# Top-2 gate dispatch on one core: the second group's first load on the scalar queue, beside the first group's last store

## The chip, the cores and the metric

The kernel runs on one core of a Trainium2 chip. The metric is the device time of one execution in microseconds; lower is better. Times before and after are medians of several runs.

## The reference

For 16 x 1024 = 16,384 tokens with 512 values each there are 8 router logits per token. The reference takes a softmax over the 8, keeps the two largest probabilities, scales them so that they sum to one, and writes the token's row twice, once times each of the two weights, the smaller first:

```python
probs = np.exp(router_logits - logits_max); probs /= probs.sum(-1, keepdims=True)
topk_indices = np.argsort(probs, axis=-1)[..., -k:]            # k = 2
topk_probs = np.take_along_axis(probs, topk_indices, axis=-1)
topk_probs = topk_probs / topk_probs.sum(-1, keepdims=True)
out = x[:, :, None, :].repeat(k, axis=2) * topk_probs[..., None]   # (16, 1024, 2, 512) float32
```

33.5 MB of x and 0.5 MB of logits are read, 67.1 MB of output are written.

## The kernel before

Tokens are laid on 128 partitions, 128 to a partition. They are cut into two groups (GROUPS = 65 and 63 tokens to a partition); a "row" below is one token on every partition. A row of x is 2 KB on a partition, a row of output 4 KB. In a group, each partition's rows lie together in memory, in x and in the output, so a transfer of n rows is one contiguous piece for each partition.

There are two big tiles in the on-chip memory. `xs` holds 65 rows of x. `osp` holds 18 rows of output. The output of a stretch is written either to `osp` or into `xs` itself, over rows of x that are used up, two places to an output row. That is why the loads of group 2 must wait for the stores of group 1 that read `xs`.

For each group the code issues loads, and then for each stretch a multiplication on VectorE and a store:

```python
LOADS = [[6, 12, 16, 31], [16, 16, 31]]
STORES = [
    [(0, 3, "osp", 0), (3, 15, "osp", 3), (18, 16, "xs", 0), (34, 15, "osp", 0), (49, 16, "xs", 33)],
    [(0, 16, "osp", 2), (16, 16, "xs", 0), (32, 15, "osp", 0), (47, 16, "xs", 32)],
]
```

An entry of STORES is first row, rows, tile and place in it. Group 1's x is at places 0 to 64 of `xs`, group 2's at 1 to 63. The first load of group 2 therefore fills places 1 to 16, the second 17 to 32, the third 33 to 63. The store (18, 16, "xs", 0) reads places 0 to 31, and the store (49, 16, "xs", 33), group 1's last, reads 33 to 64. So the first load doesn't overlap the last store, and the third load does.

The weights come from one small chain on VectorE and two sigmoids on ScalarE (`top2_weights`), early in the kernel. All loads and stores are issued from SyncE's queue (SP, queue q1), in program order, except the very first store of 3 rows, which goes over the scalar queue (ACT, queue q10). Within SP's queue, the three loads of group 2 stand behind all stores of group 1 and ahead of all stores of group 2. A multiplication that writes to place 0 of `osp` again is cut in two (FREE), since its first rows are free earlier.

Lines of the profile before: L120 is every load of x, L125 and L126 the loads of the logits, L133 the multiplication, L145 every store.

Of the kernel before, what the change touches and what calls it, by code (L numbers as in the profile page):

```python
# [1 line left out]

# [4 lines left out]

F32 = mybir.dt.float32
ALU = mybir.AluOpType
ACTF = mybir.ActivationFunctionType  # L10
P = 128


def top2_weights(nc, WA, dlt, room, logits, E):

    tt = nc.vector.tensor_tensor
    hi, lo, n = None, None, E  # L20
    while n > 1:
        n //= 2
        if hi is None:
            a, b = logits[:, :, 0:n], logits[:, :, n : 2 * n]
            nhi, nlo = room(n), b
            tt(nhi, a, b, op=ALU.max)  # L26
            tt(nlo, a, b, op=ALU.min)  # L27
        else:
            a, b = hi[:, :, 0:n], hi[:, :, n : 2 * n]
            nhi, nlo, tmp = room(n), room(n), room(n)  # L30
            tt(tmp, lo[:, :, 0:n], lo[:, :, n : 2 * n], op=ALU.max)  # L31
            tt(nlo, a, b, op=ALU.min)  # L32
            tt(nlo, nlo, tmp, op=ALU.max)  # L33
            tt(nhi, a, b, op=ALU.max)  # L34
        hi, lo = nhi, nlo
    tt(dlt, hi[:, :, 0], lo[:, :, 0], op=ALU.subtract)  # L36
    nc.scalar.activation(WA[:, :, 0], dlt, ACTF.Sigmoid, scale=-1.0)  # L37
    nc.scalar.activation(WA[:, :, 1], dlt, ACTF.Sigmoid, scale=1.0)  # L38

GROUPS = [65, 63]

LOADS = [[6, 12, 16, 31], [16, 16, 31]]
BASE = [0, 1]
# [6 lines that stand above are left out]
L = 18  # L52

FREE = [3, 2]


@with_exitstack
def kernel(
    ctx: ExitStack,
    tc: tile.TileContext,  # L60
    x: bass.AP,
    router_logits: bass.AP,
    k: bass.AP,
    out: bass.AP,
):
    nc = tc.nc
    B, S, D = x.shape
    E = router_logits.shape[-1]
    N = B * S
    assert int(k) == 2 and E == 8 and N == P * sum(GROUPS)  # L70
    M = N // P

    x_v, o_v, rl_v = [], [], []
    t0 = 0
    for n in GROUPS:
        t1 = t0 + P * n
        x_v.append(
            x.rearrange("b s d -> (b s) d")[t0:t1].rearrange("(p m) d -> p m d", p=P)
        )
        o_v.append(  # L80
            out.rearrange("b s k d -> (b s) k d")[t0:t1].rearrange(
                "(p m) k d -> p m k d", p=P
            )
        )
        rl_v.append(
            router_logits.rearrange("b s e -> (b s) e")[t0:t1].rearrange(
                "(p m) e -> p m e", p=P
            )
        )
        t0 = t1  # L90

    wpool = ctx.enter_context(tc.tile_pool(name="wpool", bufs=1))
    xs = wpool.tile([P, max(GROUPS), D], F32)
    osp = wpool.tile([P, L, 2, D], F32)
    WA = wpool.tile([P, M, 2], F32)
    dlt = wpool.tile([P, M], F32)


    flat = osp.rearrange("p l k d -> p (l k d)")
    taken = [0]  # L100

    def room(n):
        o = taken[0]
        taken[0] += M * n
        return flat[:, o : o + M * n].rearrange("p (m n) -> p m n", n=n)

    logits = room(E)

    def place(where, at, n):

        if where == "osp":
            return osp[:, at : at + n]
        return xs[:, at : at + 2 * n, :].rearrange("p (r k) d -> p r k d", k=2)

    m0 = 0
    for g, G in enumerate(GROUPS):
        x0, r = BASE[g], 0
        for n in LOADS[g]:
            tc.keep_in_program_order(
                nc.sync.dma_start(xs[:, x0 + r : x0 + r + n, :], x_v[g][:, r : r + n, :])  # L120
            )
            r += n
            if g == 0 and r == 6:
                n0 = GROUPS[0]
                tc.keep_in_program_order(nc.sync.dma_start(logits[:, :n0], rl_v[0]))  # L125
                tc.keep_in_program_order(nc.sync.dma_start(logits[:, n0:], rl_v[1]))  # L126
                top2_weights(nc, WA, dlt, room, logits, E)
        assert r == G
        for r, n, where, at in STORES[g]:
            og = place(where, at, n)  # L130
            again = where == "osp" and at == 0 and r > 0
            for a, b in [(0, FREE[g]), (FREE[g], n)] if again else [(0, n)]:
                nc.vector.tensor_tensor(  # L133
                    og[:, a:b],
                    xs[:, x0 + r + a : x0 + r + b, :]
                    .unsqueeze(2)
                    .to_broadcast([P, b - a, 2, D]),
                    WA[:, m0 + r + a : m0 + r + b, :]
                    .unsqueeze(3)
                    .to_broadcast([P, b - a, 2, D]),  # L140
                    op=ALU.mult,
                )

            queue = nc.scalar if g == r == 0 else nc.sync
            tc.keep_in_program_order(queue.dma_start(o_v[g][:, r : r + n], og))  # L145
        m0 += G


# [1 line left out]
_INS = ['x', 'router_logits', 'k']  # L150
_OUTS = [((16, 1024, 2, 512), 'float32')]

_NUMBERS = {'k': 2}


# [26 lines left out]
```

## Time and profile before

| what | value |
|---|---|
| median of 3 runs | 240.02 us (239.98 to 240.04) |
| profiled execution, its time | 240.69 us |
| its span | 238.9 us |
| VectorE busy | 141.8 us (59%) |
| ScalarE busy | 1.8 us (1%) |
| bytes moved by DMA | 101.19 MB, mean 424 GB/s over the span |
| share of sixteen DMA engines, SP's queue / ACT's queue | 97.0% / 1.5% |

The span runs from the first instruction to the last; the profiled execution's own time is 1.8 us longer. "SPq" and "ACTq" are the instruction queues of SyncE and ScalarE, and the time given for a DMA there is only its issue. The data moves later, on sixteen DMA engines that both queues share; the time "to landing" is from issue until all of the data has arrived.

### The profile page before, as it was taken

The page shows a single profiled execution, that of the slowest core. Times are in us where ns is not written, and L with a number is a line of the kernel's source. Part 1 is how long each engine was busy: PE and PEld are TensorE (multiplying, and loading weights), DVE is VectorE, ACT ScalarE, POOL GpSimd, SP SyncE. Part 2 cuts the span into 40 slices and gives each one's busy share as a digit, 9 for nine tenths or more (in the row PEclk, how much of TensorE's full clock was granted, in tenths as well). Part 3 has the DMA queues.
Part 4 walks back from the last instruction along what each step waited for, and adds up shares of the span by engine and source line. Part 5 has one row for each costly group of instructions (what it writes and reads, how often), then busy time and mean ns, then how long its engine had stood idle before and what let it go on. Part 6 is the DMA issues. An engine that isn't in the chain of part 4 may idle for free.

```text
span 238.9 us, 105 instructions
## 1 busy us (share of the span) xinstructions
DVE 141.8 (59%) x22; ACT 1.8 (1%) x3; POOL 0.2 (0%) x4
## 2 busy tenths in 40 slices
DVE  0699999980089999100000799999306999950000
ACT  2000000000000000000000000000000000000000
POOL 0000000000000000000000000000000000000000
DMA  7999998979989997989899999798989899989894
GB/s 262 439 440 430 377 544 372 494 339 494 494 362 472 406 484 339 494 351 527 351 439 439 439 433 510 340 505 362 505 373 494 384 461 395 484 350 505 362 516 176
DMA packets 2592, 101.19 MB, mean 424 GB/s; under 512 B 288, under 2 KB 416, under 8 KB 544
## 3 DMA queue, kind: packets, MB, share of 16 engines
q1 hardware_dynamic: 2448, 99.62, 97.0%
q10 hardware_dynamic: 144, 1.57, 1.5%
HBM read 34.08 MB, written 67.11 MB: 424 GB/s over the span
## 4 chain that ended last, share of the span: by engine, by line
DMA 45%; DVE 43%; SPq 0%; issue 0%; ACT 0%; DVEq 0%
DMA out_dram<-osp 27%; DVE osp L133 27%; DMA xs<-in_x_dram 15%; DVE xs L133 14%; DMA osp<-in_router_logits_dram 3%; DVE osp L26 0%; DVE osp L27 0%; DVE osp L33 0%; DVE osp L32 0%; DVE osp L34 0%; DVE osp L31 0%; SPq L125 0%; SPq L120 0%; SPq L145 0%; ACT WA L38 0%
## 5 line engine op out<-in xcount | busy, mean ns | idle before, releaser
L133 DVE TENSOR_TENSOR osp<-xs,WA 128x3072 f32<-128x3072 f32 (+5 forms) x7 | 69.3, 9907 | 62.2 <-DMA xs<-in_x_dram 36.4
L133 DVE TENSOR_TENSOR xs<-xs,WA 128x16384 f32<-128x16384 f32 x4 | 68.9, 17224 | 0.1
L26 DVE TENSOR_TENSOR osp<-osp 128x512 f32<-128x512 f32 x1 | 0.7, 693 | 8.3 <-DMA osp<-in_router_logits_dram 8.3
L37 ACT ACT_TABLE_LOAD x1 | 1.3, 1283 | 0.7 <-PEq L163 0.7
L27 DVE TENSOR_TENSOR osp<-osp 128x512 f32<-128x512 f32 x1 | 0.7, 691 | 0.0
L32 DVE TENSOR_TENSOR osp<-osp 128x256 f32<-128x256 f32 (+1 forms) x2 | 0.7, 350 | 0.0
L31 DVE TENSOR_TENSOR osp<-osp 128x256 f32<-128x256 f32 (+1 forms) x2 | 0.7, 349 | 0.0
L33 DVE TENSOR_TENSOR osp<-osp 128x256 f32<-128x256 f32 (+1 forms) x2 | 0.7, 349 | 0.0
L34 DVE TENSOR_TENSOR osp<-osp 128x256 f32<-128x256 f32 (+1 forms) x2 | 0.7, 348 | 0.0
L37 ACT ACTIVATE WA<-dlt 128x128 f32<-128x128 f32 x1 | 0.3, 315 | 10.2 <-DVE dlt L36 10.2
L36 DVE TENSOR_TENSOR dlt<-osp 128x128 f32<-128x128 f32 x1 | 0.3, 293 | 0.0
L38 ACT ACTIVATE WA<-dlt 128x128 f32<-128x128 f32 x1 | 0.3, 298 | 0.0
L163 POOL MEMSET const-bfloat16-1.0<- 128x1 bf16 x1 | 0.1, 101 | 0.0
L163 POOL MEMSET const-uint8-127<- 128x1 uint8 x1 | 0.1, 101 | 0.0
L163 POOL MEMSET const-float32-0.0<- 128x1 f32 x1 | 0.1, 98 | 0.2 <-issue 0.2
L163 POOL MEMSET const-float32-1.0<- 128x1 f32 x1 | 0.1, 98 | 0.0
## 6 DMA issues: line engine op xcount, KB each, us to landing
out_dram<-osp SPq DMA_DIRECT2D x3, 7680.0 KB, 24.4
xs<-in_x_dram SPq DMA_DIRECT2D x2, 7936.0 KB, 41.8
xs<-in_x_dram SPq DMA_DIRECT2D x3, 4096.0 KB, 35.9
xs<-in_x_dram SPq DMA_DIRECT2D x1, 3072.0 KB, 13.4
xs<-in_x_dram SPq DMA_DIRECT2D x1, 1536.0 KB, 6.1
out_dram<-osp ACTq DMA_DIRECT2D x1, 1536.0 KB, 22.2
osp<-in_router_logits_dram SPq DMA_DIRECT2D x1, 260.0 KB, 6.4
osp<-in_router_logits_dram SPq DMA_DIRECT2D x1, 252.0 KB, 6.5
```

Of the source, the lines that this page charges most:

```text
L26: tt(nhi, a, b, op=ALU.max)
L27: tt(nlo, a, b, op=ALU.min)
L31: tt(tmp, lo[:, :, 0:n], lo[:, :, n : 2 * n], op=ALU.max)
L32: tt(nlo, a, b, op=ALU.min)
L33: tt(nlo, nlo, tmp, op=ALU.max)
L34: tt(nhi, a, b, op=ALU.max)
L36: tt(dlt, hi[:, :, 0], lo[:, :, 0], op=ALU.subtract)
L37: nc.scalar.activation(WA[:, :, 0], dlt, ACTF.Sigmoid, scale=-1.0)
L38: nc.scalar.activation(WA[:, :, 1], dlt, ACTF.Sigmoid, scale=1.0)
L133: nc.vector.tensor_tensor(og[:, a:b], xs[:, x0 + r + a : x0 + r + b, :] .unsqueeze(2) .to_broadcast([P, b - a, 2, D]), WA[:, m0 + r + a : ...
L163: nc = _bacc.Bacc("TRN2", target_bir_lowering=False, num_devices=1)
```

## The change

The first load of group 2 (16 rows, places 1 to 16 of `xs`) is issued from the scalar queue instead of SP's. A dependence is added by hand: it begins when the store ahead of the last one of group 1, (34, 15, "osp", 0), has landed. All other instructions keep their queues and their order.

```diff
     m0 = 0
+    stores = []
     for g, G in enumerate(GROUPS):
         x0, r = BASE[g], 0
         for n in LOADS[g]:
-            tc.keep_in_program_order(
-                nc.sync.dma_start(xs[:, x0 + r : x0 + r + n, :], x_v[g][:, r : r + n, :])
-            )
+
+            queue = nc.scalar if g == 1 and r == 0 else nc.sync
+            load = queue.dma_start(xs[:, x0 + r : x0 + r + n, :], x_v[g][:, r : r + n, :])
+            if queue is nc.scalar:
+                tc.add_manual_dep(
+                    load.ins,
+                    stores[-2].ins.name,
+                    mybir.DependencyInfo(
+                        mybir.DependencyClass.Sync, mybir.DependencyReason.DATA
+                    ),
+                    reason="begin when the store ahead of the last has landed",
+                )
+            tc.keep_in_program_order(load)
             r += n
...
             queue = nc.scalar if g == r == 0 else nc.sync
-            tc.keep_in_program_order(queue.dma_start(o_v[g][:, r : r + n], og))
+            stores.append(queue.dma_start(o_v[g][:, r : r + n], og))
+            tc.keep_in_program_order(stores[-1])
         m0 += G
```

## The prediction

> **What bounds the kernel now.** I read the page first for which resource is full, then the waits of the engines, then the waits of SP's own queue, then the DMA issues one by one, and last the trace's single DMA packets. The page:
>
> ```profile
> span 238.9 us, 105 instructions
> DVE 141.8 (59%) x22; ACT 1.8 (1%) x3; POOL 0.2 (0%) x4
> DMA  7999998979989997989899999798989899989894
> DMA packets 2592, 101.19 MB, mean 424 GB/s; under 512 B 288, under 2 KB 416, under 8 KB 544
> q1 hardware_dynamic: 2448, 99.62, 97.0%
> q10 hardware_dynamic: 144, 1.57, 1.5%
> ```
>
> The row to look at is the DMA row: nearly full in every slice. q1 is SP's queue and q10 ACT's; together their packets took 98.5% of sixteen engines' time. VectorE is busy for 59% only. There are 18 transfers of 128 partitions, and 2592 / 18 = 144 packets each: 128 data packets, one for each partition (I call them lines), and 16 end marks of 4 bytes. So each of the 16 DMA engines has 8 lines and a mark of every transfer.
>
> I put the packets, in order of start, onto sixteen engines. They then lie back to back on every engine from 1.81 us to 237.71 us, without a gap: 235.9 us from first to last, of which the mean engine is busy for 235.5. The same line always takes the same time: 65,536 bytes (a 16-row store) 2.418 us, 61,440 bytes (15 rows) 2.267, 63,488 bytes (a 31-row load) 2.342, 32,768 bytes (a 16-row load) 1.213. The end is therefore the sum of the lines' durations, and a wait of VectorE shortens nothing unless a DMA engine runs dry because of it. The biggest wait of VectorE is the one that the change is aimed at:
>
> ```profile
> DVE osp L133 <- DMA xs<-in_x_dram: 36.4, 1, 36.4
> DVE osp L133 <- DMA out_dram<-osp: 25.3, 2, 13.6
> ```
>
> The first row is VectorE waiting for the second group's first load. The timeline of that stretch shows why it is long:
>
> ```profile
> 79.31 0.33 SPq L145 DMA_DIRECT2D out_dram<-osp  x1
> 96.57 0.33 SPq L145 DMA_DIRECT2D out_dram<-xs  x1
> 96.95 26.58 SPq L120 DMA_DIRECT2D xs<-in_x_dram  x3
> 132.90 17.23 DVE L133 TENSOR_TENSOR osp<-xs,WA 128x16384 f32<-128x16384 f32 x1 [36.36 <-DMA xs<-in_x_dram]
> 150.16 0.34 SPq L145 DMA_DIRECT2D out_dram<-osp  x1
> ```
>
> The load is issued at 96.95 and lands 35.86 us later, since two stores stand ahead of it in the same queue. The third load of that row waits on SP for the last store of group 1:
>
> ```profile
> SPq L120 <- DMA out_dram<-xs: 24.2, 1, 24.2
> ```
>
> By packets, the last store's lines run from 102.86 to 122.76, the first load's to 132.5, the second's to 142.1, the third's from 141.5 to 161.6. No engine is idle in between.
>
> **The change, part by part.** *Issue.* One 16-row load leaves SP and comes to ACT, 128x8192, 4.19 MB either way; bytes, lines and marks stay. An issue costs 0.33 to 0.37 us of the issuing queue. On SP, one issue less ahead of the second load, at 97 us, with 6 us of lines queued: nothing. On ACT the load stands behind the activations and the small store of 16.12, and waits there for the store issued at 79.31. Nothing is queued behind it on ACT, so this wait holds up no one.
>
> *When it starts.* The store of 79.31 lands 24.4 us later:
>
> ```profile
> out_dram<-osp SPq DMA_DIRECT2D x1, 7680.0 KB, 24.4
> ```
>
> That is 103.7; the load is issued by 104.1. By then the last store is on the engines, 7 to 8 of its 8 lines still to go.
>
> *How the two queues share.* The trace has one such case, the small store on ACT's queue beside loads on SP's:
>
> ```profile
> 16.12 0.37 ACTq L145 DMA_DIRECT2D out_dram<-osp  x1
> out_dram<-osp ACTq DMA_DIRECT2D x1, 1536.0 KB, 22.2
> ```
>
> With equal shares of bytes 1.57 MB would pass in 2 x 1.57 / 0.424 = 7.4 us; it took 22.2. By packets, each engine first finished three lines of SP's queue (the current one and two more, first ACT line at 19.7 to 21.1), and then took one line of each queue in turn: 0.46 us of ACT's, 1.21 or 2.34 us of SP's. So shares go by line, and the longer line gets more. Here the load has the short line, 1.21 us, and the store the long one, 2.42.
>
> The Trainium skill, "DMA: Bandwidth & Descriptors", section "Queues, rings and completion order", says that an engine drains a whole packet of a ring, some 9 to 17 descriptors typically, before it switches rows. By that rule the load's 8 lines and its mark would pass in one go and land near 120; this trace's turns of one line speak against it. The same page's section "Issuing engines are not separate DMA queues" speaks against the change altogether: a second issuer saves sequencer time only. By either rule the sum below is the same, since they shift lines and remove none.
>
> *Landing of the load.* On one engine, the store's lines start at 102.9; three go first, to 110.1. Then five turns of 1.21 + 2.42 = 3.63 us, to 128.3: the store's data is out. Three load lines are left, now in turn with the second load's lines of 1.21 us: 6 lines, 4.85 us less the part after the mark, to about 134.3. The landing came 0.9 us after this engine's mark before (132.81 against 131.88), so 135.2; with two lines first instead of three, 134.0. VectorE starts at 134 to 135.3, *later* than 132.9 by 1 to 2.5 us. The load is spread out beside the store and not moved ahead of it.
>
> *What hangs on that.* The store of group 2's first part is issued at 151.3 to 152.6 instead of 150.16. The engines need it when the third load's lines end, at 160.7 on the first engine; a queue that is ready starts within 1.1 us of the issue (0.72 to 1.81 at the kernel's start). At least 7 us of cover remain. After that the order on SP's queue is as before, and VectorE's next wait, for this store's landing at 181.23, moves by nothing.
>
> *The third load.* It waits on SP for the last store of group 1, which now lands at about 130.5 instead of 123.2, being shared. Queued behind it on SP are group 2's stores, which are not ready before 151. The engines need the third load when the first two are through, at 141.5 as before, because store and loads together are the same lines. The cover shrinks from 18 us to 11; an issue and its start cost 1.4. Whatever the arbitration, the second load lies behind the store in SP's queue, so 9.7 us (8 x 1.213) of it are always left when the store is out. If this cover were gone, each microsecond of lateness would be one at the end.
>
> *The turns themselves.* What is left is whether lines get longer where reads and writes alternate. Lines longer than usual occur in four places of the trace. At the start, 0.57 us for the mean engine, unchanged. At 18 to 28 us, where the small store runs beside the 16-row load: 0.54 us for the mean engine, 0.74 for the engine that ends last. Most of it lies on the load line before the first store line (0.25) and on the load's last line (0.24). Near 158, where the third load gives way to a store: 0.48, and 0.75 on the engine that ends last. Near 45, the same switch: 0.04. In between, from 28 to 38 us, four turns of 2.34 and 0.46 us cost nothing at all, and the switch from store to load at 122 costs nothing. The new turns begin from a store (row of 122: 0), go through six to eight load lines between store lines, and end in loads. From the 16-row load's inner lines at 20 to 25 us, 0.016 us a line, eight make 0.13. The bounds are 0 and 0.54 + 0.13 = 0.67 for the mean engine, up to 0.9 for the slowest. Below zero: the 0.48 near 158 could vanish if the engines come to that switch in another order. I take 0.25: the inner lines at 0.13 and half of one 0.24 switch.
>
> *The sum.* The profiled execution took 240.69, its span is 238.9, so 1.8 lies around it. Issue 0, landing of the load 0 (covered), third load 0 (covered), turns +0.25: 240.94 for a profiled one. The median of the runs is 240.02, 0.67 below the profiled execution; so 240.3. A measurement of this kernel can tell about 0.2%, 0.48 us, from no change; the bounds of "same" are 239.54 and 240.50.
>
> **The rivals.** The forecast, a load that lands no earlier, all of it hidden, and turns at +0.25, has a chance of 0.56.
>
> *The turns cost more (slower).* Lines that alternate pay at each switch what 18 to 28 us shows at its two bad places, about 0.24. With five or six turns that is 1.2 to 1.4: 241.3. For it: the only 16-row load that was mixed with stores has its mean line at 1.280 instead of 1.213. Against it: the four free turns from 28 to 38 us. It decides from about 0.1 us a turn (five turns make 0.48). With the milder sum of 0.67 to 0.9 the time is 240.7 to 240.9. Chance 0.32.
>
> *A gain (faster).* If the engines took the load's eight lines in one go from 110.1, it would be in 9.7 us later and land near 121, and VectorE would start 12 us earlier. That alone gives 240.0, since no engine was idle. A gain beyond 0.48 needs the long lines near 158 to go as well, with nothing paid in the turns: 240.02 - 0.48 = 239.5, at best 239.3 by the slowest engine. Chance 0.12.
>
> *The load isn't beside the store.* The dependence could hold it until the store is through; then it lands no later than 142 and VectorE's store still comes at 159.5, just in time: 240.0, within "same". The order of instructions shows it on ACT behind the store of 79.31, so this is not likely.
>
> **How the numbers follow.** Same 0.56, slower 0.32, faster 0.12. The predicted time is that of the forecast, 240.3. The range goes from the gain's 239.5 up to the dearer turns' 241.3; what is left out are turns dearer still and a dry queue. The forecast's own range is 240.0 to 240.7.
>
> **What would show it.** Right: in the profile after, VectorE's wait for the load is 37 to 39 us; ACT's load is issued near 104 and lands 30 to 31 us later; the third load is issued on SP near 130.5; the DMA row stays full, and q10 carries 5.77 MB. The lines sum to 235.5 to 236.2 for the mean engine. Wrong: a landing near 121 (the engines drain a queue in one go), a gap between lines near 141 or 160 (a cover that I overrated), or lines of 1.213 us that become 1.4 and more in the stretch from 110 to 130.

## The result and the profile after

The changed kernel took 241.39 us (median of 8 runs, 240.76 to 242.64) against 239.98 us before (8 runs, 239.85 to 240.04): a ratio of 1.0059 with a 95% interval of 1.0046 to 1.0072, so 0.6% slower. Its fastest run is slower than any run of before, and its times scatter over 1.9 us where those of before stay within 0.2. The forecast was 240.3, the range ended at 241.3.

The profiled execution took 241.52 us. Its page shows the same nearly full DMA row, with the load's 4.19 MB moved from q1 to q10:

```profile
span 239.7 us, 107 instructions
DMA  7999897979989897999989999989899999898984
DMA packets 2592, 101.19 MB, mean 422 GB/s; under 512 B 288, under 2 KB 416, under 8 KB 544
q1 hardware_dynamic: 2304, 95.42, 92.6%
q10 hardware_dynamic: 288, 5.77, 5.6%
```

The two shares add to 98.2% of a span that is 0.8 us longer; before it was 98.5%. In time that is the same: the lines' durations sum to 235.48 us for the mean engine, and to 235.52 before. So the mean DMA engine was busy no longer than before, and yet the last of them ended later.

VectorE's waits, and the timeline of the stretch around the load:

```profile
DVE osp L144 <- DMA xs<-in_x_dram: 39.4, 1, 39.4
DVE osp L144 <- DMA out_dram<-osp: 23.2, 2, 13.5
```

```profile
96.39 0.33 SPq L156 DMA_DIRECT2D out_dram<-xs  x1
96.77 34.88 SPq L122 DMA_DIRECT2D xs<-in_x_dram  x2
103.70 0.35 ACTq L122 DMA_DIRECT2D xs<-in_x_dram  x1
135.72 17.23 DVE L144 TENSOR_TENSOR osp<-xs,WA 128x16384 f32<-128x16384 f32 x1 [39.36 <-DMA xs<-in_x_dram]
152.97 0.34 SPq L156 DMA_DIRECT2D out_dram<-osp  x1
```

The load is issued from ACT at 103.70, and VectorE starts the second group at 135.72, 2.8 us later than before (132.90). SP's row of two loads ends at 96.77 + 34.88 = 131.65: the third load was issued then, 10 us before the engines needed it. The store of 152.97 also came in time. None of these waits reaches the end.

What does reach the end is in the single packets (their times, here and below, are counted from a point 0.07 to 0.09 us ahead of the timeline's zero). On thirteen engines the last data packet ends between 236.4 and 236.8 us, a little sooner than before (236.6 to 237.4 for fifteen engines there, 237.7 for the last). Three engines end at 238.1, 238.3 and 238.6. Their lines, with the start of each in us (S a 16-row store line, L a 16-row load line, L31 a line of the third load):

```
one of the thirteen   S 103.0  S 105.4  L 107.8               S 109.0  L 111.4 ... L31 158.0 (2.34)  S 160.4
late engine 1         S 103.0  S 105.4  S 107.8 (3.06)  L 110.9 (1.53)  S 112.4 ... L31 159.0 (3.20)  S 162.2
late engine 2         S 102.9  S 105.3  S 107.8 (3.19)  L 110.9         S 112.2 ... L31 158.8 (3.31)  S 162.1
late engine 3         S 103.1  S 105.5  S 107.9 (3.17)  L 111.1         S 112.3 ... L31 158.9 (3.57)  S 162.5
```

In brackets are durations; the usual ones are 2.42 (S), 1.21 (L) and 2.34 (L31). Thirteen engines turned to the load after two lines of the last store. Three took a third store line first, and this line was under way when the others changed from storing to loading and back. It took 0.64 to 0.77 us too long. From then on these engines are late, so their last line of the third load is under way when the others turn to stores at 160.4, and it takes 0.86 to 1.23 too long. For late engine 3 that is 0.75 + 1.23 = 1.98 us; it ended 2.0 us after the median engine. Between the two places, nothing is longer on any engine. Of the thirteen, six have 0.04 to 0.19 extra on their last load line near 158, where in the trace of before all sixteen had 0.16 to 0.75.

The execution's time is the last engine's end plus a constant: 241.52 - 238.56 = 2.96 after, 240.69 - 237.70 = 2.99 before, 2.96 to 2.98 in ten of the eleven profiles below, and 3.10 in that of e11. So the mean engine says nothing of the time; the slowest does.

### The profile page after: what moved, and what is told of

The parts are those of the page before. It is cut to its first block, busy times and chain, and to the rows that moved or that the text cites. A ratio compares the mean times of both kernels' runs of the same rounds, so it can differ in the third digit from the quotient of the medians.

```text
span 239.7 us, 107 instructions
## 1 busy us (share of the span) xinstructions
DVE 141.8 (59%) x22; ACT 1.8 (1%) x3; POOL 0.2 (0%) x4
## 4 chain that ended last, share of the span: by engine, by line
DMA 53%; DVE 35%; issue 0%; SPq 0%; ACT 0%; ACTq 0%; DVEq 0%
DMA out_dram<-osp 36%; DVE osp L144 27%; DMA xs<-in_x_dram 13%; DVE xs L144 7%; DMA osp<-in_router_logits_dram 3%; DVE osp L26 0%; DVE osp L27 0%; DVE osp L33 0%; DVE osp L32 0%; DVE osp L31 0%; DVE osp L34 0%; SPq L136 0%; SPq L122 0%; ACT WA L38 0%; DVE dlt L36 0%
## 5 line engine op out<-in xcount | busy, mean ns | idle before, releaser
L31 DVE TENSOR_TENSOR osp<-osp 128x256 f32<-128x256 f32 (+1 forms) x2 | 0.7, 350 | 0.0
## 6 DMA issues: line engine op xcount, KB each, us to landing
xs<-in_x_dram ACTq DMA_DIRECT2D x1, 4096.0 KB, 31.9
```

## The experiments

The theory that I took from this: the load's lines reach the engines while these choose what to do next, some engines turn a line later than the rest, and whoever is out of step at a change of direction between loading and storing pays (SPLIT, later OUT OF STEP). Its rivals: every turn between a store line and a load line costs something (TURNS), or the coming of a second queue costs one long line, whatever the lines are (ARRIVAL).

| kernel | us, median (range, runs) | before beside it | ratio, 95% interval | profiled: last engine's end / median engine's |
|---|---|---|---|---|
| e1 the change again | 241.50 (240.86 to 242.85, 10) | 240.15 | 1.0062, 1.0039 to 1.0085 | 239.3 / 236.6 |
| e2 load ahead, on SP | 240.55 (240.27 to 241.42, 10) | 240.15 | 1.0016, 1.0002 to 1.0030 | 237.8 / 236.7 |
| e3 second load on ACT | 240.14 (239.86 to 241.56, 10) | 240.15 | 0.9996, 0.9976 to 1.0015 | 237.2 / 236.7 |
| e4 change, four activations | 242.37 (239.67 to 242.69, 10) | 240.15 | 1.0052, 1.0015 to 1.0088 | 239.7 / 236.6 |
| e5 before, first store on SP | 240.50 (240.39 to 240.71, 11) | 240.10 | 1.0014, 1.0005 to 1.0023 | 237.7 / 237.0 |
| e6 e4 with first store on SP | 240.27 (240.09 to 240.58, 11) | 240.10 | 1.0001, 0.9992 to 1.0011 | 237.1 / 236.9 |
| e7 change, eight activations | 242.41 (242.38 to 242.58, 4) | 240.10 | 1.0091, 1.0077 to 1.0105 | 239.5 / 236.5 |
| e8 change without dependence | 242.48 (242.18 to 243.40, 4) | 240.10 | 1.0098, 1.0077 to 1.0120 | 239.2 / 237.0 |
| e9 before again | 240.02 (239.82 to 240.28, 10) | 240.21 | 0.9988, 0.9976 to 1.0000 | 237.0 / 236.6 |
| e10 change with first store on SP | 241.19 (240.25 to 241.54, 10) | 240.21 | 1.0030, 1.0015 to 1.0045 | 238.6 / 237.1 |
| e11 store beside the store | 240.45 (240.34 to 242.23, 10) | 240.21 | 1.0022, 0.9999 to 1.0045 | 237.4 / 236.9 |

**e1, the change again.** No edit.

> The changed kernel once more, for a second profile. Three theories. SPLIT: the load's lines reach the engines while these choose their next line; some engines get them one line later than the rest, go on storing while the others already read, lose about 0.7 us there, are then late, and lose about 1 us more where the third load gives way to a store near 158. The end is set by those few engines. Expected: again a few engines (not the same number as before, perhaps) with one line longer by 0.6 to 0.8 us near 108, the same engines with a last load line longer by 0.8 to 1.3 near 158, ends of the engines spread over 1.5 us or more; time 240.7 to 242.7, scattered. TURNS: every turn between a store line and a load line costs something on every engine; expected long lines all through 108 to 130 us on all engines, and a steady time. ARRIVAL: the coming of a second queue's lines costs each engine one long line, whatever the lines are; expected long lines near 108 on most engines.

```profile
104.16 0.35 ACTq L122 DMA_DIRECT2D xs<-in_x_dram  x1
```

Again slow and scattered; the profiled execution took 242.29. Here it was a single engine. It came 0.7 us late to the last store (first line at 103.7 instead of 103.0) and turned after two store lines, the other fifteen after three. Its store line of 113.3 took 0.52 too long, two more 0.10 each, and its last load line 1.19, from 159.7, 0.6 to 1.0 us before the others turned to stores. The fifteen others had no long line after 47 us. TURNS and ARRIVAL, which want long lines on all or most engines, are against this.

**e2, the load ahead of the last store, in SP's own queue.**

```diff
+            if g == 1 and r == 0:
+                r += n
+                continue
...
+            if g == 0 and r + n == G:
+                tc.keep_in_program_order(
+                    nc.sync.dma_start(xs[:, 1 : 1 + LOADS[1][0], :], x_v[1][:, 0 : LOADS[1][0], :])
+                )
             tc.keep_in_program_order(queue.dma_start(o_v[g][:, r : r + n], og))
```

> The same load moved ahead of group 1's last store in SP's own queue, none of it on ACT. VectorE then starts group 2 near 114 instead of 132.9. SPLIT: in one queue all engines have the same order of lines, none can be a line off; 239.9 to 240.3, steady, engines' ends within 1.1 us of each other as before the change. TURNS: one more switch from loads to a store than before, 240.0 to 240.5. ARRIVAL: no second queue there, 240.0. If an idle VectorE were what bounds the kernel, this would be the fastest of all, by up to 10 us; none of the three expects that.

```profile
85.52 0.34 SPq L150 DMA_DIRECT2D xs<-in_x_dram  x1
96.44 0.33 SPq L152 DMA_DIRECT2D out_dram<-xs  x1
...
113.78 17.23 DVE L136 TENSOR_TENSOR osp<-xs,WA 128x16384 f32<-128x16384 f32 x1 [17.37 <-DMA xs<-in_x_dram]
```

In this timeline VectorE starts group 2 at 113.78, 19 us earlier than before, and the kernel gains nothing: 240.55, 0.16% slower. That settles that VectorE's long wait was covered, and that the aim of the change brings nothing here even where it is reached. But one queue for all is not without late engines: the engine that ends last, 1.1 us after the median one, lost 0.53 and 0.16 us near 105 and 112, around the added switch, 0.26 at 134 and 0.30 at 159.

**e3, the second load on ACT instead, after the last store.**

```diff
-            queue = nc.scalar if g == 1 and r == 0 else nc.sync
+            queue = nc.scalar if g == 1 and r == 16 else nc.sync
...
-                    stores[-2].ins.name,
+                    stores[-1].ins.name,
```

> The first load of group 2 is back on SP; the second one (also 16 rows) goes over ACT, when group 1's last store has landed. So the second queue's lines arrive beside load lines, with no turn between loads and stores. SPLIT: some engines may take the new lines one line later, but all read either way, so nothing is lost: 239.9 to 240.3, steady, no long lines from 122 to 145. TURNS: 240.0 as well. ARRIVAL: as the change, 240.7 and more, with long lines near 126. The first load now lands near 139 and VectorE's store is issued near 156, still ahead of the third load's end at 160.

No change, 240.14 against 240.15. The lines of the two queues alternate just the same, load beside load. Four engines have one line longer by 0.1 to 0.3 near 124.8, the others none in that stretch, and the last engine ends 0.5 after the median one, by a last load line near 158 that took 0.53 too long. ARRIVAL falls. In this profile all engines took four lines first, so it does not show a split without cost; e11 does.

**e4, the change with four activations ahead of the load.** They shift the issue by 1.4 us.

```diff
+                for i in range(4):
+                    steps.append(nc.scalar.activation(dlt, dlt, ACTF.Sigmoid))
...
-                    stores[-2].ins.name,
+                    steps[-1].ins.name,
```

The first of them waits for the store ahead (stores[-2]), the load for the last of them.

> The changed kernel, with four small activations on ScalarE between the landing of the store ahead and the issue of the load (they overwrite a tile that nobody reads again). The issue moves from 103.7 to about 105.2, so that the lines arrive near the middle of a store line (these begin at 103.0, 105.4, 107.9) instead of where the engines choose. SPLIT: all engines take the load after the same number of store lines, here three; no few engines with a line longer by 0.6; time 239.9 to 240.5 and steady to 0.3. TURNS: as the change, 240.7 to 242.6 (there are as many turns but one). ARRIVAL: as the change.

```profile
104.45 1.33 ACT L125 ACTIVATE dlt<-dlt 128x128 f32<-128x128 f32 x4 [91.67 <-DMA out_dram<-osp]
105.81 0.35 ACTq L136 DMA_DIRECT2D xs<-in_x_dram  x1
```

Half a hit. The times fall into two bands with nothing between: four runs at 239.67 to 240.06, as fast as before, and six at 242.36 to 242.69. So the median, which stands in the upper band, says little here, and the ratio of 1.0052 is not that of the medians (1.0092). The profiled execution (242.69) is of the upper band, with a cause that I had not reckoned with. All engines took three store lines, so the split is gone. But one engine came 1.0 us late, at 104.1. It had been late by 0.4 from the kernel's second load on, and had lost more between 18 and 48 us. Five of its lines at 111 to 127, a load line and four store lines, took 0.12 to 0.76 too long, 1.6 together, and one of its last load lines 0.55. The fast band already speaks against TURNS, since the kernel and its turns are the same there, though no execution of that band was profiled.

**e5, the kernel before with its first store on SP too.**

```diff
-            queue = nc.scalar if g == r == 0 else nc.sync
+            queue = nc.sync
```

> The kernel before, with its very first store (3 rows) on SP's queue too, so that nothing is issued from ACT. The profiles so far show one engine that starts its second load about 0.4 us late, and is 0.4 to 1.0 us late after the stretch from 18 to 36 us, in which this store's lines alternate with load lines. OUT OF STEP (what became of SPLIT): an engine that stores while most of the others load, or loads while they store, gets longer lines; so whoever is late is made later at every turn, and the slowest engine sets the end. Expected: no long lines from 18 to 28, the late engine no later than 0.5 before the stores begin, time 239.2 to 239.8, 0.2 to 0.8 below the kernel before. TURNS (each turn costs, on every engine): also faster, by the 0.5 of that stretch. If that stretch is worth nothing: 240.0 to 240.2.

A miss: 240.50, 0.14% slower and not faster. The long lines from 18 to 28 us are gone, but every engine's last load line near 41 us, ahead of that store, now takes 0.6 to 1.4 too long, 1.0 in the mean. So it looks as if the first change from loads to stores has a cost of its own, which moved with the change; this comparison alone doesn't separate it from that of the early alternation.

**e6, e4 and e5 together.**

> The changed kernel with the four small activations ahead of the load, and the first store on SP's queue. With the activations alone the times fell into two bands, 239.7 to 240.1 (4 of 10) and 242.4 to 242.7 (6 of 10), and the profile of a slow one showed an engine that came 1.0 us late to the alternating lines. OUT OF STEP: without the early alternation the late engine is at most 0.4 to 0.5 late, less than half a load line, so the upper band gets rarer or vanishes; median 239.2 to 240.1. TURNS: 241 to 242, one band. If the lateness comes from elsewhere: both bands as before.

```profile
104.00 1.33 ACT L125 ACTIVATE dlt<-dlt 128x128 f32<-128x128 f32 x4 [91.28 <-DMA out_dram<-osp]
105.36 0.37 ACTq L136 DMA_DIRECT2D xs<-in_x_dram  x1
135.38 17.23 DVE L158 TENSOR_TENSOR osp<-xs,WA 128x16384 f32<-128x16384 f32 x1 [38.67 <-DMA xs<-in_x_dram]
```

The timeline shows the load issued at 105.36. The upper band is gone: eleven runs within 0.5 us, 240.27, ratio 1.0001. In the packets all sixteen engines begin the last store within 103.1 to 103.6, take three of its lines, and then alternate load and store lines in step. From 80 to 236 us not one line on any engine is longer than usual, and all engines end within 236.6 to 237.1. The load runs beside the last store here, from the other queue, with five turns to and fro, at no cost. TURNS falls.

**e7, eight activations,** otherwise as e4.

> As with four activations, but eight: the issue moves to about 107.1, so the lines arrive near the next moment at which the engines choose (107.8), and some take three store lines first and others four. OUT OF STEP: as the change, 240.7 to 242.7, scattered, a few engines a line apart with lines longer by 0.5 to 0.8 near 110. TURNS: one turn less than the change, 240.7 to 242. If only the amount of alternation counts, less than the change, 240.3 to 240.6.

```profile
103.54 2.69 ACT L125 ACTIVATE dlt<-dlt 128x128 f32<-128x128 f32 x8 [90.98 <-DMA out_dram<-osp]
106.27 0.34 ACTq L136 DMA_DIRECT2D xs<-in_x_dram  x1
```

242.41, slow as expected, but not scattered: the four runs lie within 0.2. Fifteen engines took four store lines before the load, and one, whose lines began last (103.2), took three. That one lost 0.50, 0.46, 0.18 and 0.10 in its store lines at 111.6 to 123.7 and 1.54 in its last load line, 2.8 us in all, and ended 2.9 after the median engine. The kernel has fewer turns than e6, counting from where the load sets in, and is 2.1 us slower. (Its first store is still on ACT, unlike e6's. The nearer comparison is the fast band of e4, 239.67 to 240.06.)

**e8, the change without the dependence added by hand.**

```diff
-                tc.add_manual_dep(
-                    load.ins,
-                    stores[-2].ins.name,
...
```

> The changed kernel without the dependence added by hand: the load is issued from ACT as soon as the places it fills are free, near 85.5, and its lines alternate with the lines of the store ahead (15 rows, 2.27 us each, from 84.7) instead of the last one. It lands near 113 to 116. OUT OF STEP: the store begins at 84.7 and the load is issued 0.8 us later, as in the change (102.9 and 103.7), so again some engines are a line apart: 240.6 to 242.6, scattered. If it was the place beside the last store, or the third load's wait for that store, that cost the time: 240.0 to 240.3.

```profile
85.53 0.33 ACTq L122 DMA_DIRECT2D xs<-in_x_dram  x1
96.42 0.33 SPq L149 DMA_DIRECT2D out_dram<-xs  x1
96.80 38.57 SPq L122 DMA_DIRECT2D xs<-in_x_dram  x2
118.77 17.23 DVE L137 TENSOR_TENSOR osp<-xs,WA 128x16384 f32<-128x16384 f32 x1 [22.38 <-DMA xs<-in_x_dram]
```

In this timeline the load is issued at 85.53 and VectorE starts at 118.77, 14 us earlier than before, and the kernel is among the slowest of all: 242.48. Six engines turned to the load after two lines of the 15-row store, ten after three. The six lost 0.2 to 0.6 in each of two or three store lines at 94 to 103, five of them 0.9 to 1.2 near 112 (one 0.4), and ended at 238.9 to 239.2, the ten at 236.6 to 237.4. The ten weren't free of long lines: each lost 0.2 to 0.8 in one to three load lines between 109 and 115. So neither the place beside the last store nor the third load's wait made the cost. This profile also narrows the theory. The six late engines begin their last line of the third load at 160.5 to 160.8, the ten others begin to store at 160.5 to 161.3, and the six lines take their usual 2.34. So here reading while the others stored cost nothing by itself, and neither did a line that began about when the others turned. The late engines' long lines at this place began earlier: 1.3 to 2.0 us before the others' turn in the profile of the change, 0.6 to 1.1 in e1 and e7. What fits these profiles is that a line pays when it is well under way *while the others change direction*.

**e9, the kernel before again.** No edit.

> The kernel before, unchanged, for a second profile. In the first one all sixteen engines had a longer last load line near 158 (0.48 us for the mean engine), and that execution took 0.67 us more than the median of the runs. OUT OF STEP has no place for that: all engines were loading. If it was chance in that one execution, this profile has little there (under 0.2 for the mean engine) and a time near 240.1; one engine some 0.4 to 1.0 late from the first 36 us on, as in the other profiles, and ends spread by 1 to 1.5 us. If it belongs to the kernel, again 0.4 to 0.5 near 158.

240.02. The long lines near 158 are there again but smaller, 0.19 for the mean engine instead of 0.48, with the ends within 0.6 us of each other. Why they vary from one execution to the next while the engines are nearly in step stays open. The first profiled execution was 0.67 us above the median because its last engine ended at 237.7; here the last ends at 237.0.

**e10, the change with the first store on SP.** The edit is e5's.

> The changed kernel with the first store on SP's queue, without the activations. In the kernel with both, all engines were within 0.5 us of each other at 103 and took the load after the same three store lines, with not one long line, and 240.27. Here only the moment of the arrival is that of the change again. OUT OF STEP: the arrival falls again where the engines choose, some take two store lines first and some three; 240.7 to 242.6. If only the engine that comes late from the early stretch makes the cost, it is gone here too: 240.1 to 240.5.

```profile
104.35 0.37 ACTq L122 DMA_DIRECT2D xs<-in_x_dram  x1
```

241.19, slow without the help of the early alternation: five engines took three store lines where eleven took two; one of the eleven began the store 0.5 us late. The five lost 0.1 to 0.6 us a line at 108 to 116. They and the late one then lost 0.3 to 1.2 near 159 and ended at 237.8 to 238.6, the other ten by 237.1. One thing doesn't fit: one of the six and one of the other ten began this line within 0.01 us of each other, at 158.7, and only the one of the six lost anything (0.72).

**e11, a store beside the store.** All loads are on SP, and the last store is cut in three.

```diff
+                for a, b in [(0, 6), (6, 12)]:
+                    tc.keep_in_program_order(nc.sync.dma_start(o_v[g][:, r + a : r + b], og[:, a:b]))
+                part = nc.scalar.dma_start(o_v[g][:, r + 12 : r + n], og[:, 12:n])
+                tc.add_manual_dep(
+                    part.ins,
+                    stores[-1].ins.name,
...
```

> All loads on SP. Group 1's last store is cut into three: two of 6 rows on SP, and one of 4 rows on ACT, which waits for the same landing as the load of the change did, and so comes at the same moment beside SP's lines. All of the alternating lines are stores. OUT OF STEP: engines may differ by a line and one may be late, but all write; no long lines from 104 to 122, 239.9 to 240.4. If the alternation of two queues, or the engines' being a line apart, costs by itself, whatever the direction: 240.7 to 242.6.

```profile
96.35 1.42 SPq L149 DMA_DIRECT2D out_dram<-xs  x2
97.86 25.98 SPq L122 DMA_DIRECT2D xs<-in_x_dram  x3
103.58 0.34 ACTq L150 DMA_DIRECT2D out_dram<-xs  x1
```

The timeline shows ACT's store issued at 103.58, as the load of the change. In the packets one engine, 0.3 to 0.5 us behind the rest, took five of SP's lines first, and the fifteen others six: a split. From 104 to 121 us no line on any engine is longer than usual. A split between two queues that both store costs nothing in those lines, as expected. The median is 240.45; but three of ten took 241.4 to 242.2, and they weren't profiled, so what happened in them stays open. The interval reaches from no change to 0.45% slower.

## Why the prediction was wrong

**What bounds the kernel: right.** The lines on the engines set the end, and VectorE's wait was covered: e2 and e8 start VectorE 19 and 14 us earlier and gain nothing.

**Issue, share and landing: right, a little short.** ACT's load was forecast near 104 and came at 103.70; it landed after 31.9 us (forecast 30 to 31):

```profile
xs<-in_x_dram ACTq DMA_DIRECT2D x1, 4096.0 KB, 31.9
```

The engines did take one line of each queue in turn, as the small store of before had shown, and not the load's eight lines in one go. VectorE started at 135.7; 134 to 135.3 was forecast. The late engines set this too: the thirteen had their last line of the load by 132.3, the three at 133.9 to 134.2, and the landing came at 135.6. (In the working of the landing, "6 lines, 4.85 us" should be five lines, 6.07 us; the stated 134.3 follows from that.) The third load went out at 131.65 (130.5 forecast). The DMA engines never ran dry.

**The turns: wrong, and this is the step that failed.** The text took +0.25 us, between bounds of 0 and 0.67 for the mean engine, "up to 0.9 for the slowest"; the kernel lost 1.41. For the mean engine the change cost -0.04 (235.48 against 235.52); in that sense even 0.25 was too much. But the end is set by the slowest engine, and this one moved from 237.7 to 238.6 in the profiles, and to 239.3 in the second one. Even the 0.9 was too small: the first profile of before took 0.67 us more than the median of its runs, and from e9's, which took just the median, to the profile of the change the slowest engine moved by 1.5 us (237.0 to 238.6). The sum was added up over the wrong engine, although the ends of all sixteen, 236.6 to 237.7, lay open in the trace of before. None of the signs named for a wrong prediction came up but one load line of 1.53 us; they looked at the load's landing, at gaps and at the load's own lines, and not at the spread of the ends.

Behind that is a wrong choice of rows. The new turns were priced by the switch from store to load at 122 us (0), by the inner lines of the early load at 20 to 25 us (0.13) and by half of one early switch, and the free turns from 28 to 38 spoke against more. At 122 us the engines move in step, and in the other places the store lines are short (0.46 us). What the change adds is a second queue with long lines that sixteen engines do not all turn to after the same line. The forecast worked out the landing for three store lines first and for two, and did not ask what happens if some engines take two and some three. Its own figure for the small store, a first ACT line "at 19.7 to 21.1", was such a split: nine engines began by 20.3, seven at 21.0 or later, one load line on. The rival "the turns cost more" ended nearer to the time (241.3), but that is luck: its mechanism, a price on every turn, is refuted by e6.

**What is shown, and what isn't.** That the cost comes with the engines' being out of step is shown by a pair of kernels that differ only in four small activations, and so in the moment of the issue: e6 against e10 (the same lines and queues; issued at 105.36 and at 104.35 in the profiles; 240.27 and 241.19). e6 against e7 agrees (all engines at three lines, or one at three and fifteen at four: 240.27 and 242.41; the first store's queue differs too), and so does every profile of a load beside a store above 241 us: the engines that end late are those that took another number of lines or came late, and they lost most in long lines. That in the upper band of e4 and in the unprofiled executions it is always the same thing is likely and not shown. Why a line gets longer when it straddles the others' change of direction is not shown by anything here, and being out of step isn't the only thing that lengthens lines: in the trace of before all sixteen engines, nearly in step, lost 0.16 to 0.75 near 158.

The Trainium skill, "DMA: Bandwidth & Descriptors", section "Issuing engines are not separate DMA queues", says that issuing from several engines at once only saves the sequencers' time. The runs agree that there is nothing to gain; they add that there can be something to lose, 0.6% here and 1.0% in e8.

## What to carry to other kernels

Where the DMA engines are full, an idle compute engine is no reason to reorder transfers: first ask whether any DMA engine would run dry, and e2 shows what the answer is worth. Seven profiles here have a load on a second queue beside a store. In five of them the engines did not all turn to it after the same line, in a sixth (e4) one engine came late, and those out of step set the end; only in e6 were all in step, at no cost. On one queue (e2) or beside a transfer of the same direction (e3, e11) the median stayed within 0.2% of before; three unprofiled executions of e11, at 241.4 to 242.2, keep this from being a rule. Add up the slowest engine and not the mean one, and look into a new scatter of the times (here 1.9 us instead of 0.2) before you put it down to the measurement.

## What the hardware showed that I had not expected

The moment of the issue counts to within about a microsecond: with the first store on SP, the same load issued at 104.35 made the kernel 241.19 and at 105.36 240.27; with that store on ACT, issued at 106.27, 242.41. After the issue an engine took the line it was at and one or two more of the other queue before its first line of the load: in the profile of the change the load was issued at 103.70, and its first lines began at 107.7 to 108.1 on thirteen engines and at 110.9 to 111.1 on three.

In the profiles of before, e1 and e4, one engine was 0.3 to 0.4 us later than the median one already in the kernel's second load. In the kernel before, the last engine ended 0.8 us after the median one; with long lines of opposite direction in two queues the lateness grew to 2.7 us in e1 and 3.1 in e4.

The first change from loads to stores costs every engine 0.6 to 1.4 us in e5, in the load line that is under way, where the later ones cost an engine nothing or up to 0.6.
